# Last down-projection steps by columns, shorter norm sums, down loads in order of use, and the first head's q and k staged earlier

## The chip, the cores and the metric

The kernel runs on one core of one Trainium2 chip. The core has TensorE (matmuls and transposes, called PE in the profile), VectorE (DVE), ScalarE (ACT), GpSimd (POOL) and SyncE (SP, which here only issues DMAs). SBUF is the working memory, PSUM holds the results of matmuls. The metric is device time in microseconds of one execution, and lower is better; several runs are given by their median.

## The reference, cut to what matters

A trunk of two layers over 1024 rows of width 1024, in float32. Layer 0 mixes rows by a gated block, layer 1 by attention of 16 heads; each then has a gated ConvFFN with its own norm before it, and a final norm ends the trunk.

```python
def rmsnorm(x, g):
    return x * lax.rsqrt(jnp.mean(x * x, axis=-1, keepdims=True) + EPS) * g

def conv_ffn(h, w_in, conv_w, conv_b, w_down):          # D_FF = 2816
    a = causal_conv3(h @ w_in, conv_w) + conv_b
    up, gate = jnp.split(a, 2, axis=-1)
    return (jax.nn.silu(gate) * up) @ w_down

h = x
h = h + gmlp_mixer(rmsnorm(h, a_norm_g), ...)            # mixer A
h = h + conv_ffn(rmsnorm(h, f_norm_g[0]), ...)
k, v = jnp.split(rmsnorm(h, kv_norm_g) @ w_kv, 2, -1)
h = h + chunk_attention(rmsnorm(h, b_norm_g), k, v, w_q, rel_bias, w_o)
h = h + conv_ffn(rmsnorm(h, f_norm_g[1]), ...)
return rmsnorm(h, final_norm_g)
```

## The kernel before

**Layout and precision.** The residual `h` lies transposed in SBUF: eight tiles of 128 features by 1024 rows, handled as two halves of 512 rows, t = 0 and t = 1. A float32 operand is split into a rounded high part (`whi`, `yh`: a copy on ScalarE, L137) and the rest (`wlo`, `yl`: a subtraction, L138, mostly on VectorE), and a product takes three matmuls: high by high, low by high, high by low.

**Order of the work.** TensorE's instructions run in the order of the program text. Of the other engines and of SyncE's queue the program's scheduler sets the order when the kernel is built, except in blocks marked `manual_schedule`. Work that must not hold TensorE up is put off: `put_off(us, fn)` runs `fn` when a clock that counts the matmuls issued so far (`tick`: columns/2400 us + 0.0025) has passed that many us. `tc.issue_after(ins)` puts the block's instructions behind `ins` on that engine.

**Norms.** For each half, `square_sum` squares every new tile of `h` on ScalarE (L217, L220) and adds the squares into two tiles `acc[0]` and `acc[1]`, odd tiles on VectorE and even ones on GpSimd. `rstd_rows` adds the two on VectorE (L226), and 0.9 us of the clock later TensorE sums over the features with four small products (L231, eight matmul instructions, `pm`). The mean (L197), the power -1/2 on GpSimd (L198), a diagonal tile (L204) and a product with ones (`bc`, L207) follow, then the scaled tiles `y` (L243) and their splits.

**Down projection.** `down` multiplies by one level of a seven-product block scheme: seven products p in the order 1, 6, 2, 7, 5, 4, 3, each with 11 steps q, 77 steps in all. A step is twelve matmuls of 512 columns: four output blocks m ("columns" here), each three matmuls, into four PSUM banks. Two steps' operands come with one pair of loads on SyncE (L799 for the weights' part `d`, L800 for the activations' part `g`) into eight buffers; the splits are made some three steps ahead, and the pair `whi`, `wlo` has four buffers. For the first 24 steps ScalarE, VectorE and SyncE keep the text's order; after that the scheduler's. When p = 4 ends, half t = 0 of `h` is complete and `after(0, ...)` starts its norm during p = 3; when p = 3 ends, half t = 1 is. In layer 0 that is the norm for attention, in layer 1 the final norm.

**The first head.** After layer 0's `down`, TensorE makes the first pair of heads' q, k, v of t = 0, then v, q, k of t = 1. Then `first` splits them (L960 to L967), and `stage(0)` copies them by six DMAs (L999) into the operand tiles QE, QS, KM, KS. The pass for the row maxima (`Max`, L1021 to L1032) reads them first.

**The end.** In the final norm `rows` transposes blocks of `h` back (`back`, L1283), scales and stores (`store`, L1288). For t = 1, `gain` makes transposed blocks times the gain beforehand, and `last` scales and stores them.

Of the kernel before, what the change touches and what calls it, by code (L numbers as in the profile page):

```python
# [46 lines left out]
def trunk(ctx: ExitStack, tc: tile.TileContext, x, a_win, a_wv, a_wst, a_bs, a_wout, w_kv, w_q, w_o,  # L47
# [174 lines left out]

    def rstd_rows(acc, pool, then, n=4):

        cs = slice(0, n * P)
# [40 lines left out]
    def norm(h, acc, t, gain, ys):  # L266
# [8 lines left out]
        put_off(4.2 if t else 3.2, lambda: rstd_rows(acc, npl, lambda r: put_off(2.9 if t else 6.0, lambda: scale(r))))  # L275
# [18 lines left out]
    def norm_first(h, acc, gain, X):  # L294
# [11 lines left out]
        put_off(3.2, lambda: rstd_rows(acc, npl, lambda r: put_off(6.0, lambda: scale(r))))  # L306

    def norm_second(h, acc, gain, X):
# [40 lines left out]
        put_off(4.6, lambda: rstd_rows(acc, npl, lambda r: put_off(3.6, lambda: scale(r))))  # L349
# [38 lines left out]
    with tc.tile_pool(name="a1", bufs=1, reuse_waits="tile") as a1, \  # L388
# [152 lines left out]
        def out_a(t, gs, room=None):  # L541
            hs = halves[t]
            acc = new_acc(npl)
# [238 lines left out]
    def down(l, gs, ds, hold, after):  # L782

        wd = f_wdown[l].rearrange("(q e p) c -> p q e c", e=2, p=P)
        with tc.tile_pool(name=f"dx{l}", bufs=4, reuse_waits="tile") as dx, \
# [4 lines left out]
            ready, raw, sets = [], {}, [0]  # L790

            def load(p, q):
# [6 lines left out]
                nc.sync.dma_start(d[:, :n, :], src[p] if p in src else ds[LEFT[p]][:, q:q + n, :])  # L799
                nc.sync.dma_start(g[:, :n, :], gs[RIGHT[p]][:, q:q + n, :])  # L800
# [13 lines left out]
            s1, acc = [None] * 4, [None, None]  # L814
            bank = {b: [psum[n][i][:, hs] for hs in halves for n in ("up", "gate")] for i, b in enumerate("ab")}
            for n, (p, q) in enumerate(steps):
# [8 lines left out]
                (wh, wl), (xh, xl) = ready[n]  # L825
                ready[n] = True
                b = "a" if p in (1, 2, 5, 3) else "b"
                first, last = q == 0 and p in (1, 6, 5, 4), q == NP - 1
# [5 lines left out]
                if not last:  # L834
                    continue
# [59 lines left out]
    for what in "qkv":  # L895
        proj(ps2[what, 0], w2[what], ys[0])
# [515 lines left out]
```

## Time and profile before

| what | value |
|---|---|
| median of 3 runs | 2236.21 us (2229.96 to 2240.26) |
| the profiled execution: its own time | 2239.42 us |
| its span in the trace | 2237.2 us |
| mean granted clock of TensorE | 0.988 |
| busy in the span: PE, DVE, ACT, POOL | 2162.8, 1583.7, 1081.2, 728.2 us |

A profile is of one execution: the span goes from its first instruction to its last, and the time of the execution is 2.2 us longer. The rows of the trace count us from the start of the span. The stages lie as follows: mixer A to about 300 us, layer 0's ConvFFN to 736, its `down` to 960, first q, k, v to 1005, attention to 1500, its output product to 1560, layer 1's ConvFFN to 1994, its `down` to 2219, then the end.

### The profile page before, as it was taken

Reading aid. Unit: us, or ns where it says so; the run is one execution under the profiler, and the core shown is the slowest. Engines: PE = TensorE matmul, PEld = TensorE weight load, DVE = VectorE, ACT = ScalarE, POOL = GpSimd, SP = SyncE. Lnnn points to the kernel's source line nnn. Section 1 sums busy time; section 2 is a strip of 40 time slices with the busy share of each in tenths; the row PEclk is TensorE's granted clock in tenths of the full one; section 3 lists DMA queues with packets and bytes.
Section 4 is the critical chain, followed back from the end, with each engine's and each line's share of the span. In section 5 each row is a group of like instructions: output and inputs, shape, how many; then the busy total and the mean of one; then the engine's idle time right before and its main releaser. Section 6 shows DMA issues by size and latency. Waiting matters only on the chain.

```text
span 2237.2 us, 28258 instructions
## 1 busy us (share of the span) xinstructions
PE 2162.8 (97%) x9880; PEld 1785.8 (80%) x9880; DVE 1583.7 (71%) x2406; ACT 1081.2 (48%) x1909; POOL 728.2 (33%) x487
## 2 busy tenths in 40 slices
PE   8999999999999999998999999999999999999997
PEld 7888887888888887777888888787778888888876
DVE  4763869888888665654767776664988888885555
ACT  6544445454454543444555555552544444455432
POOL 0311316424234112153444444352543333240111
PEclk9999999999999999999999999999999999999998
DMA  5242224444445865335444444653244444477652
GB/s 203 85 141 76 90 99 146 168 144 164 143 170 186 316 234 189 122 116 125 109 113 115 113 123 123 179 170 152 85 160 168 148 162 162 156 255 278 211 174 80
DMA packets 151054, 344.04 MB, mean 154 GB/s; under 512 B 31744, under 2 KB 32128, under 8 KB 150912
## 3 DMA queue, kind: packets, MB, share of 16 engines
q1 hardware_dynamic: 148176, 337.31, 46.4%
q10 hardware_dynamic: 2736, 4.93, 0.6%
q8 instruction: 77, 1.26, 0.2%
q14 instruction: 65, 0.53, 0.1%
HBM read 225.20 MB, written 87.56 MB: 140 GB/s over the span
## 4 chain that ended last, share of the span: by engine, by line
PE 48%; DVE 20%; issue 18%; DMA 8%; POOL 3%; ACT 3%; SPq 0%; DVEq 0%; ACTq 0%; POOLq 0%
DVE wlo L138 6%; PE vps L468 4%; DMA raw<-in_f_win 3%; PE up L357 3%; PE up L359 3%; PE up L362 3%; DVE a L707 3%; PE qkv L186 3%; PE qkv L182 2%; PE qkv L179 2%; PE gate L357 2%; PE gate L359 2%; DVE S L372 2%; PE gate L362 2%; PE up L832 2%
## 5 line engine op out<-in xcount | busy, mean ns | idle before, releaser
L138 DVE TENSOR_TENSOR wlo<-raw,whi 128x512 fp32r<-128x512 f32 x425 | 370.0, 888 | 181.4 <-ACT whi L137 181.1
L137 ACT CAST whi<-raw 128x512 fp32r<-128x512 f32 x429 | 262.7, 626 | 231.4 <-PE gate L832 110.3
L357 PE MATMUL up<-yh,whi 128*128 128x512 f32 x688 | 269.9, 392 | 6.8 <-ACT gate L760 6.6
L359 PE MATMUL up<-yh,wlo 128*128 128x512 f32 x688 | 268.0, 390 | 0.0
L1081 POOL TENSOR_TENSOR pl<-p,ph 128x640 fp32r<-128x640 f32 (+4 forms) x128 | 163.8, 1283 | 203.6 <-ACT ph L1080 109.9
L721 POOL TENSOR_TENSOR h<-a 128x512 f32<-128x512 f32 x44 | 80.1, 1820 | 368.2 <-DVE a L713 368.2
L357 PE MATMUL gate<-th,whi 128*128 128x512 f32 x496 | 193.4, 390 | 5.0 <-DVE gate L774 3.1
L359 PE MATMUL gate<-th,wlo 128*128 128x512 f32 x496 | 193.0, 389 | 0.0
L138 DVE TENSOR_TENSOR yl<-raw,yh 128x512 fp32r<-128x512 f32 x180 | 126.1, 734 | 94.1 <-ACT yh L137 93.9
L362 PE MATMUL up<-yl,whi 128*128 128x512 f32 x688 | 184.5, 389 | 0.5 <-POOL yl L138 0.5
L137 ACT CAST yh<-raw 128x512 fp32r<-128x512 f32 x184 | 105.8, 617 | 117.9 <-DMA raw<-gT 95.2
L357 PEld LDWEIGHTS up<-yh,whi 128*128 128x128 f32 x688 | 129.1, 188 | 40.9 <-ACT gate L760 14.3
L362 PEld LDWEIGHTS up<-yl,whi 128*128 128x128 f32 x688 | 129.1, 188 | 28.3 <-POOL yl L138 1.3
L359 PEld LDWEIGHTS up<-yh,wlo 128*128 128x128 f32 x688 | 129.2, 188 | 26.3
L182 PE MATMUL qkv<-yh,wlo 128*128 128x512 f32 x336 | 134.8, 401 | 0.0
L179 PE MATMUL qkv<-yh,whi 128*128 128x512 f32 x336 | 133.0, 396 | 0.0
L362 PE MATMUL gate<-tl,whi 128*128 128x512 f32 x496 | 132.6, 389 | 0.0
L137 ACT CAST whi<-S 128x512 fp32r<-128x512 f32 x160 | 99.0, 620 | 63.3 <-PE up L362 58.1
L832 PE MATMUL up<-yh,wlo 128*128 128x512 f32 x308 | 122.0, 396 | 6.7 <-DVE wlo L138 6.6
L832 PE MATMUL up<-yh,whi 128*128 128x512 f32 x308 | 121.6, 395 | 1.8 <-ACT whi L137 1.8
L138 DVE TENSOR_TENSOR wlo<-S,whi 128x512 fp32r<-128x512 f32 x160 | 121.3, 759 | 0.0
L832 PE MATMUL up<-yl,whi 128*128 128x512 f32 x308 | 121.2, 394 | 0.0
(253 smaller groups left out, 5330.6 us busy)
## 6 DMA issues: line engine op xcount, KB each, us to landing
raw<-in_f_win SPq DMA_DIRECT2D x88, 512.0 KB, 3.6
gT<-h SPq DMA_DIRECT2D x88, 256.0 KB, 2.7
h<-in_f_wdown SPq DMA_DIRECT2D x44, 512.0 KB, 4.5
dS<-h SPq DMA_DIRECT2D x88, 256.0 KB, 2.1
raw<-dS SPq DMA_DIRECT2D x40, 512.0 KB, 3.5
raw<-gT SPq DMA_DIRECT2D x40, 512.0 KB, 5.2
gB<-a SPq DMA_DIRECT2D x66, 256.0 KB, 2.1
raw<-in_f_wdown SPq DMA_DIRECT2D x30, 512.0 KB, 5.4
```

Source lines behind the costliest of these rows:

```text
L137: S.copy(hi, src)
L138: return eng.tensor_tensor(lo, src, f32(hi), op=ALU.subtract)
L179: nc.tensor.matmul(ps, wh[:, k, :], xs[k][0], start=k == 0, stop=False)
L182: nc.tensor.matmul(ps, wl[:, k, :], xs[k][0], start=False, stop=False)
L186: nc.tensor.matmul(ps, wh[:, k, :], xs[k][1], start=False, stop=k == last)
L357: nc.tensor.matmul(ps, wh[:, k, :], xs[k][0], start=first and k == 0, stop=False, skip_group_check=True)
L359: nc.tensor.matmul(ps, wl[:, k, :], xs[k][0], start=False, stop=False, skip_group_check=True)
L362: nc.tensor.matmul(ps, wh[:, k, :], xs[k][1], start=False, stop=k == 3, skip_group_check=True)
L468: nc.tensor.matmul(ps, a, b, start=k == i == 0, stop=k == KD - 1 and i == 2)
L721: G.tensor_tensor(B[n], x, B.get(y) if isinstance(y, str) else y, op=ALU.subtract)
L832: nc.tensor.matmul(ps, w[:, ms], x, start=first and i == 0, stop=last and i == 2, skip_group_check=True)
L1081: marks[2] = G.tensor_tensor(pl[:, :n], pf[:, :n], f32(ph[:, :n]), op=ALU.subtract)
```

## The change

Five edits. (1) `square_sum` leaves only tile 2's addition on GpSimd, merges the two sums when tile 6 is in, and adds tile 7 to the merged sum; `rstd_rows` has no addition and no delay of its own, and the times of its callers are new. (2) In layer 1 the last four steps of p = 3 are done column by column, twelve matmuls to a column, and each column's result is added to `h` and squared right behind it (`whole`). (3) Each pair of down loads is put behind the pair before it in SyncE's queue. (4) The first head's operand tiles are opened before its q, k, v; half t = 0 of q and k is split and staged ahead of the products of t = 1, half t = 1 right behind them, and KM goes first. (5) In the end, the four `gain` blocks of t = 1 are made during p = 3, `last` scales them on ScalarE and stores them from ScalarE's queue, and the other four go through `rows` on VectorE and SyncE's queue.

`operand`, `stage` and `constant_rows` are moved out of the attention block with little change; lines that only move are cut.

```diff
@@ -207,31 +207,28 @@
-    def new_acc(pool, bufs=2):
-        return [pool.tile([P, H], F32, tag="acc", name="acc", bufs=bufs) for _ in range(2)]
+    accs = [2]
 
     def square_sum(acc, h, m, pool):
 
-        a = acc[m % 2][:, 0:h.shape[1]]
         if m < 2:
-            S.activation(a, h, AF.Square)
-        else:
-            sq = pool.tile([P, H], F32, tag="f", name="sq")[:, 0:h.shape[1]]
-            S.activation(sq, h, AF.Square)
-            (V if m % 2 else G).tensor_tensor(a, a, sq, op=ALU.add)
-
-    def rstd_rows(acc, pool, then, n=4):
-        behind["sum"] = V.tensor_tensor(acc[0][:, cs], acc[0][:, cs], acc[1][:, cs], op=ALU.add)
-
-        def rows():
-            pt = psS("pm")
-            for i in range(n):
-                nc.tensor.matmul(pt[:, i:i + 1], acc[0][:, i * P:(i + 1) * P], ones[:, 0:1], start=True, stop=True)
-                tick(0)
-            then(rstd_of(pt[:, :n], n, pool))
-        put_off(0.9, rows)
+            acc.append(pool.tile([P, H], F32, tag="acc", name="acc", bufs=accs[0]))
+            S.activation(acc[m], h, AF.Square)
+            return
+        sq = pool.tile([P, H], F32, tag="f", name="sq")
+        S.activation(sq, h, AF.Square)
+        a = acc[0 if m == KD - 1 else m % 2]
+        (G if m == 2 else V).tensor_tensor(a, a, sq, op=ALU.add)
+        if m == KD - 2:
+            V.tensor_tensor(a, a, acc[1], op=ALU.add)
+
+    def rstd_rows(acc, pool, then):
+
+        pt = psS("pm")
+        for i in range(4):
+            nc.tensor.matmul(pt[:, i:i + 1], acc[0][:, i * P:(i + 1) * P], ones[:, 0:1], start=True, stop=True)
+            tick(0)
+        then(rstd_of(pt[:, :4], 4, pool))
...
-        put_off(4.2 if t else 3.2, lambda: rstd_rows(acc, npl, lambda r: put_off(2.9 if t else 6.0, lambda: scale(r))))
+        put_off(8.5 if t else 6.0, lambda: rstd_rows(acc, npl, lambda r: put_off(2.9 if t else 6.0, lambda: scale(r))))
...
-        put_off(3.2, lambda: rstd_rows(acc, npl, lambda r: put_off(6.0, lambda: scale(r))))
+        put_off(4.0, lambda: rstd_rows(acc, npl, lambda r: put_off(6.0, lambda: scale(r))))
...
-        put_off(4.6, lambda: rstd_rows(acc, npl, lambda r: put_off(3.6, lambda: scale(r))))
+        put_off(3.6, lambda: rstd_rows(acc, npl, lambda r: put_off(3.2, lambda: scale(r))))
...
+            end = 4 if l else 1
...
-                nc.sync.dma_start(d[:, :n, :], src[p] if p in src else ds[LEFT[p]][:, q:q + n, :])
-                nc.sync.dma_start(g[:, :n, :], gs[RIGHT[p]][:, q:q + n, :])
+                with tc.issue_after(behind["down"].ins) if sets[0] > 1 else ExitStack():
+                    nc.sync.dma_start(d[:, :n, :], src[p] if p in src else ds[LEFT[p]][:, q:q + n, :])
+                    behind["down"] = nc.sync.dma_start(g[:, :n, :], gs[RIGHT[p]][:, q:q + n, :])
...
+            s1, acc = [None] * 4, [[], []]
+
+            def whole(p, m, ps):
...
+                V.tensor_tensor(x, ps, x, op=ALU.add)
+                square_sum(acc[t], x, k, npl)
...
+                if n > len(steps) - end:
+                    continue
+                todo = range(n, n + end if n == len(steps) - end else n + 1)
                 for m in range(4):
                     ps, ms = bank[b][m], slice(m * P, (m + 1) * P)
-                    for i, (w, x) in enumerate(((wh, xh), (wl, xh), (wh, xl))):
-                        nc.tensor.matmul(ps, w[:, ms], x, start=first and i == 0, stop=last and i == 2, skip_group_check=True)
-                        tick()
-                if not last:
+                    for k in todo:
+                        q = steps[k][1]
+                        (wh, wl), (xh, xl) = ready[k]
+                        for i, (w, x) in enumerate(((wh, xh), (wl, xh), (wh, xl))):
+                            nc.tensor.matmul(ps, w[:, ms], x, start=q == i == 0 and p in (1, 6, 5, 4),
+                                             stop=q == NP - 1 and i == 2, skip_group_check=True)
+                            tick()
+                    if q == NP - 1 and len(todo) > 1:
+                        whole(p, m, ps)
+                for k in todo:
...
+                if len(todo) == 1:
+                    for m in range(4):
+                        whole(p, m, bank[b][m])
...
+    bt_ctx, b0_ctx = ExitStack(), ExitStack()
+    bt = bt_ctx.enter_context(tc.tile_pool(name="bt", bufs=2, reuse_waits="tile"))
+    b0 = b0_ctx.enter_context(tc.tile_pool(name="b0", bufs=1, reuse_waits="tile"))
+
+    QE, QS, KM, KS = ([b0.tile([P, T], F32R, name=f"{n}0")] for n in ("qe", "qs", "km", "ks"))
+
+    def constant_rows(c, places):
+        oth = rows[c][1]
+        for tl, off in ((QE[c], P), (KM[c], P + T)):
+            for hs in halves:
+                e = places()
+                nc.sync.dma_start(e[oth], consts[oth, off + hs.start:off + hs.stop])
+                S.copy(tl[oth, hs], e[oth])
...
+        if what == "q":
+            S.mul(hi[:, hs], ps, 0.125)
+            V.scalar_tensor_tensor(lo[:, hs], ps, 0.125, f32(hi[:, hs]), op0=ALU.mult, op1=ALU.subtract)
+        elif what == "k":
+            S.copy(hi[:, hs], ps)
+            V.tensor_tensor(lo[:, hs], ps, f32(hi[:, hs]), op=ALU.subtract)
...
+    def stage(hd, cs=slice(0, T)):
+
+        p, c = divmod(hd, 2)
+        own, oth = rows[c]
+        q, k = parts[p, "q"], parts[p, "k"]
+        if cs.start == 0:
+            G.memset(f32(QE[c][own.stop % P:own.stop % P + 1, :]), 0.0)
+        for dst, src in ((KM[c][own], k[0]), (QE[c][own], q[0]), (QS[c][own], q[0]), (QS[c][oth], q[1]),
+                         (KS[c][own], k[1]), (KS[c][oth], k[0])):
+            nc.sync.dma_start(f32(dst[:, cs]), f32(src[own, cs]))
+
+    def first(what, t):
+
+        for _ in operand(0, what, None, t):
+            pass
...
-    w2 = {"q": weights(0, "q"), "k": weights(0, "k"),
-          "v": weights(0, "v", wv_ctx.enter_context(tc.tile_pool(name="wv", bufs=1, reuse_waits="tile")))}
+    wv = wv_ctx.enter_context(tc.tile_pool(name="wv", bufs=1, reuse_waits="tile"))
+    w2 = {what: weights(0, what, wv if what == "v" else None) for what in "qkv"}
     for what in "qkv":
         proj(ps2[what, 0], w2[what], ys[0])
+    constant_rows(0, lambda: wv.tile([P, H], F32, tag="e", name="e", bufs=4))
+    first("q", 0)
+    first("k", 0)
+    stage(0, halves[0])
     proj(psv[:, H:T], w2["v"], ys[1])
     for what in "qk":
         ps2[what, 1] = psS("qk")
         proj(ps2[what, 1], w2[what], ys[1])
+        first(what, 1)
+    stage(0, halves[1])
...
+        constant_rows(1, lambda: b2.tile([P, H], F32, tag="o", name="e"))
...
-        def first(what, t):
-            for _ in operand(0, what, w2[what], t):
-                pass
-        for what, t in (("q", 0), ("k", 0), ("q", 1), ("k", 1), ("v", 0), ("v", 1)):
-            first(what, t)
-        stage(0)
+        for t in range(2):
+            first("v", t)
...
-    def store(n, i, j, o):
-        nc.sync.dma_start(out[n * H + i * P:n * H + (i + 1) * P, halves[j]], o)
+    def store(n, i, j, o, queue=nc.sync):
...
-        gained = {}
-
-        def gain(i, j):
-            ps = back(1, i, j)
-            gained[i, j] = new_o()
-            V.tensor_tensor(gained[i, j], ps, fg[j], op=ALU.mult)
+        def gain(i):
+
+            ps = back(1, i, 1)
+            gained.append(new_o())
+            V.tensor_tensor(gained[i], ps, fg[1], op=ALU.mult)
 
         def last(r):
             for i in range(4):
-                for j in (1, 0):
-                    if (i, j) not in gained:
-                        gain(i, j)
-                    o = gained[i, j]
-                    if j:
-                        V.tensor_scalar(o, o, r[:, i:i + 1], None, op0=ALU.mult)
-                    else:
-                        S.mul(o, o, r[:, i:i + 1])
-                    store(1, i, j, o)
+                S.mul(gained[i], gained[i], r[:, i:i + 1])
+                store(1, i, 1, gained[i], nc.scalar)
+                rows(r, i, 0)
         if n:
-            put_off(0.5, lambda: [gain(i, 1) for i in range(4)])
             put_off(1.6, lambda: rstd_rows(acc, npl, last))
         else:
-            put_off(3.2, lambda: rstd_rows(acc, npl, lambda r: [
+            put_off(6.0, lambda: rstd_rows(acc, npl, lambda r: [
                 put_off(2.9 + 0.6 * i, lambda i=i: rows(r, i // 2, i % 2)) for i in range(8)]))
+            for i in range(4):
+                put_off(16.0 + 0.8 * i, lambda i=i: gain(i))
```

## Rows read from the trace of the kernel before

**Rows 1.** Waits of TensorE, 800 to 1030 us: engine, line, releaser: total us, times, longest.
```profile
PE mx L1021 <- DMA km<-thi: 6.5, 1, 6.5
PE pm L231 <- DVE acc L226: 5.7, 2, 3.5
PE up L832 <- DVE wlo L138: 3.6, 6, 1.8
PE up L832 <- ACT whi L137: 0.9, 1, 0.9
```
**Rows 2.** The same view, 1690 us to the end.
```profile
PE pm L231 <- DVE acc L226: 7.2, 2, 4.8
PE up L832 <- DVE wlo L138: 3.0, 5, 1.5
```
**Rows 3.** The same view, whole span.
```profile
PE gate L357 <- DVE gate L774: 3.1, 2, 1.6
```
**Rows 4.** Busy time by stretch: us, each engine (x instructions), granted clock, DMA share, GB/s.
```profile
750.00:800.00 50.00, 50.00 (x222) 41.40 (x222) 26.13 (x40) 23.58 (x42) 5.19 (x5) 1.00 0.83 304
898.00:905.00 7.00, 5.16 (x16) 3.79 (x15) 4.82 (x8) 3.22 (x6) 1.27 (x1) 0.76 0.94 330
928.00:936.00 8.00, 5.81 (x23) 4.44 (x22) 4.15 (x6) 0.70 (x2) 1.87 (x2) 0.79 0.17 51
957.00:968.00 11.00, 9.42 (x34) 6.99 (x33) 6.89 (x8) 4.75 (x8) 7.80 (x4) 0.84 0.61 203
968.00:981.00 13.00, 9.48 (x31) 7.17 (x30) 7.01 (x7) 0.68 (x2) 8.66 (x5) 0.74 0.43 140
1009.00:1021.00 12.00, 5.50 (x18) 4.28 (x17) 1.45 (x8) 0.60 (x1) 1.90 (x1) 0.72 1.02 232
2184.00:2192.00 8.00, 5.60 (x22) 4.39 (x21) 4.09 (x6) 0.88 (x2) 1.80 (x2) 0.79 0.11 33
2229.00:2237.00 8.00, 1.99 (x10) 1.59 (x8) 3.54 (x8) 2.67 (x4) 0.00 (x0) 0.50 0.69 262
```
**Rows 5.** Timeline, SyncE's queue and ScalarE, 860 to 880 us: start, us, instruction [idle before].
```profile
862.35 2.19 SPq L799 DMA_DIRECT2D raw<-in_f_wdown  x2
865.86 6.23 SPq L800 DMA_DIRECT2D raw<-gT  x2
875.48 2.18 ACT L137 CAST yh<-raw 128x512 fp32r<-128x512 f32 x4 [9.44 <-DMA raw<-gT]
```
**Rows 6.** Timeline of VectorE and GpSimd, 2179 to 2189 us.
```profile
2183.56 2.57 DVE L221 TENSOR_TENSOR acc<-acc,sq 128x512 f32<-128x512 f32 x2
2186.65 0.69 DVE L226 TENSOR_TENSOR acc<-acc 128x512 f32<-128x512 f32 x1
2181.79 2.99 POOL L221 TENSOR_TENSOR acc<-acc,sq 128x512 f32<-128x512 f32 x2 [23.80 <-ACT sq L220]
```
**Rows 7.** Timeline of VectorE, TensorE and SyncE's queue, 2216 us to the end.
```profile
2218.50 1.29 DVE L850 TENSOR_TENSOR h<-up,h 128x512 f32<-128x512 f32 x2 [8.85 <-PE up L832]
2220.90 2.48 DVE L1309 TENSOR_TENSOR o<-fin,fg 128x512 f32<-128x512 f32 x4
2224.87 0.69 DVE L226 TENSOR_TENSOR acc<-acc 128x512 f32<-128x512 f32 x1
2225.71 1.77 PE L231 MATMUL pm<-ones,acc 128*128 128x1 f32 x8 [4.81 <-DVE acc L226]
2229.59 4.47 SPq L1288 DMA_DIRECT2D out<-o  x8
```
**Rows 8.** Timeline of VectorE, 968 to 992 us; SyncE's queue at 1009; ScalarE at 2208.
```profile
981.17 1.88 DVE L243 TENSOR_TENSOR y<-h,bc 128x512 f32<-128x512 f32 x3 [3.17 <-PE bc L207]
989.92 0.69 DVE L138 TENSOR_TENSOR yl<-y,yh 128x512 fp32r<-128x512 f32 x1 [0.69 <-ACT yh L137]
...
1009.54 1.04 SPq L999 DMA_DIRECT2D km<-thi  x1
...
2208.30 0.62 ACT L137 CAST whi<-raw 128x512 fp32r<-128x512 f32 x1 [2.10 <-PE gate L832]
```

More of the change, by code (lines that the diff above doesn't have):

```diff
@@ L812, in make @@
                 ready.append((w, x))
-            s1, acc = [None] * 4, [None, None]
+            s1, acc = [None] * 4, [[], []]
+            def whole(p, m, ps):
+                (h11, h12), (h21, h22) = ([h[i][:, hs] for hs in halves] for i in (m, m + 4))
+                if p == 1:
+                    s1[m] = du.tile([P, H], F32, tag="s1", name="s1", bufs=4)
+                    S.copy(s1[m], ps)
+                    return
+                if p in (6, 7):
+                    u = du.tile([P, H], F32, tag="u", name="u")
+                    V.tensor_tensor(u, ps, s1[m], op=ALU.add)
+                    for x in ((h12,) if p == 6 else (h21, h22)):
+                        G.tensor_tensor(x, x, u, op=ALU.add)
+                    return
+                x, t, k = {2: (h11, 0, m), 5: (h22, 1, m), 4: (h21, 0, m + 4), 3: (h12, 1, m + 4)}[p]
+                V.tensor_tensor(x, ps, x, op=ALU.add)
+                square_sum(acc[t], x, k, npl)
+            accs[0] = 4
             bank = {b: [psum[n][i][:, hs] for hs in halves for n in ("up", "gate")] for i, b in enumerate("ab")}
@@ L885, in trunk @@
     osave = dp.tile([2, KD, P, T], F32, name="osave")
+    rows = [(slice(0, 64), slice(64, P)), (slice(64, P), slice(0, 64))]
     def weights(p, what, pool=None):
@@ new lines, in trunk, with operand @@
+    parts = {}
+    def operand(p, what, w, t):
+        hs = halves[t]
+        if t == 0:
+            if what == "v":
+                parts[p, what] = [b1.tile([P, NB, 64], F32R, tag=f"v{n}", name=f"v{n}") for n in ("hi", "lo")]
+            else:
+                parts[p, what] = [bt.tile([P, T], F32R, tag=f"t{n}", name=f"t{n}") for n in ("hi", "lo")]
+        hi, lo = parts[p, what]
+        if p == 0:
+            ps = ps2[what, t]
+        else:
+            ps = psP("qkv")
+            yield from products(ps, w, ys[t], range(KD), LAST)
+        if what == "q":
[4 more added lines that the diff above has]
+            V.tensor_tensor(lo[:, hs], ps, f32(hi[:, hs]), op=ALU.subtract)
+        else:
+            vT = b2.tile([P, H], F32, tag="vT", name="vT")
+            S.copy(vT, ps)
+            put_off(1.2, lambda: transpose_v(vT, t, hi, lo))
@@ L910, in trunk @@
     os_ = [[None] * KD, [None] * KD]
-    rows = [(slice(0, 64), slice(64, P)), (slice(64, P), slice(0, 64))]
     def psO(name):
@@ L989, in transpose_v @@
                 V.tensor_tensor(vl, src, f32(vh), op=ALU.subtract)
-        def stage(hd):
-            p, c = divmod(hd, 2)
-            own, oth = rows[c]
-            q, k = parts[p, "q"], parts[p, "k"]
-            G.memset(f32(QE[c][own.stop % P:own.stop % P + 1, :]), 0.0)
-            for dst, src in ((QE[c][own], q[0]), (KM[c][own], k[0]), (QS[c][own], q[0]), (QS[c][oth], q[1]),
-                             (KS[c][own], k[1]), (KS[c][oth], k[0])):
-                nc.sync.dma_start(f32(dst), f32(src[own]))
         def stage_v(p):
@@ L1285, in back @@
         return ps
-    def store(n, i, j, o):
-        nc.sync.dma_start(out[n * H + i * P:n * H + (i + 1) * P, halves[j]], o)
+    def store(n, i, j, o, queue=nc.sync):
+        queue.dma_start(out[n * H + i * P:n * H + (i + 1) * P, halves[j]], o)
     def new_o():
         return yp.tile([P, H], F32, tag="yh", name="o")
+    gained = []
     def final(n, acc):
```

66 lines of the change are left out of this document (9 added, 57 removed).

## The prediction

> **What bounds the kernel now.** TensorE is busy 2162.8 of 2237.2 us, so 74 us are idle, and only what takes idle time away, or the slow matmuls behind it, can help. I read the granted clock first (0.988), then TensorE's waits, then the busy time by stretch around each wait, then the timelines of the engine that each wait names. Three kinds of wait lie where the change works: the products `pm` wait for the sums of squares, the matmuls of `down` wait for split weights, and the first head's row maxima wait 6.5 us for one copy of k [rows 1, 2]. The reader is to see that the waits are late hand-overs, one after the other, and not a lack of throughput: in the first part of `down` TensorE does 222 matmuls in 50 us without a gap [rows 4], so the pace is 0.225 us.
>
> A wait costs more than its idle time. In the stretches with the longer waits the granted clock averages 0.72 to 0.84 instead of 1.00 [rows 4], a mean over the levels 2.4 and 1.2 GHz, and matmuls at the lower one take twice as long. So I price each wait by its stretch: length minus starts times the pace, where a `pm` product counts 0.11 us (eight take 1.77 us in the end, where the clock stands at 0.50 [rows 4, 7]) and a `bc` product 0.45, my estimate, as two ordinary ones.
>
> - a, `pm` in layer 0's p = 3: 8 us, 15 matmuls and 8 `pm`: 8 - 3.4 - 0.9 = 3.7 lost.
> - b, the same in layer 1: 14 and 8: 8 - 3.2 - 0.9 = 3.9.
> - c, `pm` of t = 1 behind layer 0's `down`: 21, 8 and 2 `bc`: 13 - 4.7 - 0.9 - 0.9 = 6.5.
> - d, the first q weights: 11 - 34 x 0.225 = 3.3.
> - e, the row maxima: 12 - 18 x 0.225 = 7.9 [all rows 4].
>
> **Sums (edit 1).** VectorE's last group gets five additions where it had three (tiles 4 and 6 come from GpSimd; the merge moves ahead of tile 7). At 0.6 us a place that is 1.2 us more. Against this, VectorE's two additions took 2.57 us while GpSimd's two ran for 2.99 beside them [rows 6]; two clean ones in a row take 1.29 [rows 7], so 1.3 us come back when GpSimd's go. By the count alone the sum is ready 1.2 us later, with that excess gone about as early as now.
>
> The Trainium skill, SBUF — State Buffer, Who interferes with whom, says that a VectorE instruction with two SBUF inputs and a GpSimd instruction that reads SBUF exclude each other. By that rule the excess goes whole and the total below would be about 0.6 higher; by the bare count it would be 2.4 lower. The trace agrees with the rule in the 2.57 against 1.29.
>
> The products themselves move on the clock from 3.2 + 0.9 to 6.0, some 2.0 us of matmuls. The idle times are 5.7 - 3.5 = 2.2 for a and 7.2 - 4.8 = 2.4 for b [rows 1, 2], so 0.2 and 0.4 us stay idle, with the sums as early as now: a and b give 3.5 each. Should the sums come 1.2 us later, about half of each price stays, so each lies between 1.5 and its whole price.
>
> For c the products move from 5.1 to 8.5, 3.6 us against an idle 3.5 [rows 1]: the 6.5 go. But `bc` now comes 53 matmuls into the 72 of t = 0, and 19 matmuls, 4.3 us, lie between it and the product that reads the new tiles. Making the eight tiles took from 981.17 to 990.61 [rows 8]; the last one's high part, some 8.8 us behind `bc`, is wanted after 14 more matmuls, at 7.5. That puts back 1.3 us: c gives 5.2, between 3 (the tiles another 2 us later, since the first head's splits are now on the same engines) and 6.5.
>
> d keeps its chain: a buffer freed by the last split of `down`, the load, the gain, the split. All that moves earlier with TensorE. If it did not, the wait would grow by what a gives. I take 0, with -3 to +3. For the other norms, `norm_second` starts 2.3 us of the clock earlier, and VectorE is then behind in the ConvFFN, where TensorE waits 3.1 us for it [rows 3]; half of it, 1.5, with 0 to 3.1 (term j).
>
> **Loads in order (edit 3).** ScalarE sits 9.44 us idle before four casts for one `gT` load: its queue was filled with two weight loads at 862.35, and the second `gT` came 6 us behind the first [rows 5]. The weight casts queued behind these casts then are late, and TensorE waits. Where the order of use holds by hand, in the first 24 steps, there is no wait: 222 matmuls in 50 us at a DMA share of 0.83 [rows 4]. In layer 0 the waits are 3.6 + 0.9; the longest, 1.8, lies in a stretch that loses 7 - 16 x 0.225 = 3.4, so 6.1 in all (f) [rows 1, 4]; in layer 1 they are 3.0 (g) [rows 2]. Some of them stand beside GpSimd's long additions at the ends of p = 7 and p = 5, which stay; I take two thirds: 4.0 and 2.0, with 0 and all as the bounds.
>
> **The first head (edit 4).** The copy of k was issued at 1009.54 [rows 8] and ended the wait about 7 us later. The maxima begin on half t = 0, whose copies now go out some 20 us ahead. Block 4 is the first to want t = 1, 3.4 us behind block 0; k's last product ends near 1005, so a copy issued at 1006 lands about 1013, just ahead of that. If the queue holds it to 1009.54 again, 3.1 us of wait and a slow stretch come back. e lies between 3.4 and 7.9; I take 6.4, as VectorE's work on eight blocks is what is late next. The four casts and four subtractions for q and k were there before, and so were the constant rows; they only come earlier, under 24 matmuls each (5.4 us) of products.
>
> **The end (edits 2 and 5).** From the first addition at 2218.50 to `pm` at 2225.71 pass 7.2 us: four additions to `h`, four `gain` multiplications of 2.48, squares, and the sums [rows 7]. By columns one addition, one square and one sum stay behind the last matmul: about 0.7 + 0.6 + 0.7, 0.3 for handing over, and 0.5 because the first addition had not waited for the last bank, 2.8 in all: 4.4 saved. `pm` may keep the full clock, 0.9; I count 0.6. Eight stores of 256 KB are 2.1 MB, at 262 GB/s [rows 4] 8 us, which is all the time from the first issue at 2229.59 [rows 7] to the end at 2237.2: so the end follows the first store, and h is 5.0, between 4 and 6.5 (if the issuing, 4.47 us on one queue [rows 7], were what counts).
>
> The Trainium skill, DMA: Bandwidth & Descriptors, Issuing engines are not separate DMA queues, says that issuing from a second engine saves issue time only, because all run on the same 16 DMA engines. By it the 6.5 isn't reached. No row of before has two queues at once in the end.
>
> The sixteen transposes of `gain` were hidden under that wait; in p = 3 they cost TensorE 16 x 0.11 = 1.8 (term i). The column order needs step 76's weights nine matmuls, 2.0 us, behind step 72, whose buffer they take: a cast of 0.62 [rows 8] and a subtraction of 0.69 [rows 6] make 1.3. It is hidden with 0.7 to spare; without the cover it costs 1 us.
>
> **Sum.** 3.5 + 3.5 + 5.2 + 0 + 6.4 + 4.0 + 2.0 + 5.0 - 1.8 + 1.5 = 29.3 us off 2239.42, the profiled execution, gives 2210.1. The median of the runs is 3.2 below that execution, so I predict 2207. All upper bounds together give 3.7 + 3.9 + 6.5 + 3 + 7.9 + 6.1 + 3.0 + 6.5 - 1.8 + 3.1 = 42, all lower ones 1.5 + 1.5 + 3 - 3 + 3.4 + 0 + 0 + 4 - 1.8 + 0 = 9.
>
> **Rivals.**
> 1. The next thing is late. The loads' order frees nothing (f and g 0), the new tiles and the second half of k come late (c 3, e 3.4), d grows by 3: 3.5 + 3.5 + 3 - 3 + 3.4 + 5.0 - 1.8 + 1.5 = 15, 2221. For it: VectorE is busy 7 of 13 us in c's stretch and the copies' queue was full. Against it: the pauses are of several causes, which need not all move.
> 2. Slower: strict order blocks SyncE's queue. A weight load waits for a buffer that TensorE's pace frees, the `g` load behind it waits too, and every pair comes late. With 27 pairs behind step 24 in each `down` a wait of 1 us a pair is 54 us: with f and g 0, 2236 - 23 + 54 = 2267. It turns the sign from 23 / 54 = 0.43 us a pair. For it: the 9.44 us [rows 5] show how far one late load reaches. Against it: the first 24 steps run so without a gap [rows 4].
> 3. The loads were not the cause, the rest holds: f and g 0, 2213, inside the range.
>
> **How the numbers follow.** Forecast and rival 3 together 0.65 (its own range 2196 to 2215), rival 1 0.22, rival 2 0.07, no change that shows 0.06. The range is 2195 to 2226: from the upper bounds to rival 1 with its spread. A measurement of this kernel tells about 0.5%, 11 us, from no change: faster 0.84 (a few cases of rival 1 fall short), same 0.10, slower 0.06.
>
> **What would show it.** Right: no wait of `pm` over 1 us, none of `mx` for `km` over 3, weight waits in `down` below 3 us in all, `pm` in the end some 2.5 us behind the last matmul. Wrong: loads further apart with TensorE waiting at every second step; waits of `v` for `yh`, or of the maxima's transposed row for VectorE, of several us; or a longer attention stage, which the change does not touch but whose order the scheduler makes anew, and which this sum leaves as it is.

## The result

The changed kernel takes 2215.36 us (median of 5 runs, 2211.32 to 2221.08) against 2236.21 (5 runs, 2229.96 to 2240.26): a ratio of 0.9912 with a 95% interval of 0.9888 to 0.9935, some 20 us. The forecast was 2207. The profiled execution took 2217.12 us; its span is 2215.3, the granted clock 0.993, TensorE is busy 2152.2 us.

**The profile after.** First the waits of TensorE over the whole span (engine, line, releaser: us in total, times, longest), to be held against [rows 1 to 3].

```profile
PE up L853 <- DVE wlo L138: 10.1, 6, 2.7
...
PE gate L354 <- ACT h L695: 5.5, 4, 2.1
...
PE pm L229 <- DVE acc L221: 4.6, 3, 2.3
...
PE qk L179 <- ACT whi L137: 2.3, 1, 2.3
...
PE mx L1054 <- DMA km<-thi: 1.5, 1, 1.5
PE v L179 <- ACT yh L137: 1.5, 3, 0.6
...
PE qk L182 <- DVE wlo L138: 1.3, 1, 1.3
```

The first head's wait for `km`, 6.5 us before, is gone: the 1.5 us above stand at 1400 us, in a later head. The waits of `pm` are down from 12.9 to 4.6 us. But `up` waits 10.1 us for `wlo`, more than the 6.6 before [rows 1, 2], and the tiles of t = 1 are late three times (`v` for `yh`). The end, on VectorE, TensorE and the two queues that store (start, us, instruction, idle before it):

```profile
2201.73 0.68 DVE L829 TENSOR_TENSOR h<-gate,h 128x512 f32<-128x512 f32 x1
2203.17 0.69 DVE L221 TENSOR_TENSOR acc<-acc,sq 128x512 f32<-128x512 f32 x1 [0.76 <-ACT sq L219]
...
2204.01 1.02 PE L229 MATMUL pm<-ones,acc 128*128 128x1 f32 x8 [2.32 <-DVE acc L221]
...
2207.19 3.02 SPq L1317 DMA_DIRECT2D out<-o  x4
...
2208.39 1.78 ACTq L1317 DMA_DIRECT2D out<-o  x2
```

One addition and one sum stand behind the last matmul, and `pm` waits 2.32 us where it waited 4.81 [rows 7]. From `pm` to the end pass 11.3 us (2204.01 to 2215.3), before 11.5.

Where the time went, stage by stage. The bounds are the starts of the first or last matmul of a kind; the last column is the prediction's sum for the stage.

| stage | before | after | difference | predicted |
|---|---|---|---|---|
| ConvFFN, layer 0 | 435.5 | 433.3 | -2.3 | j, 1.5 for both |
| `down`, layer 0 | 223.4 | 224.4 | **+1.0** | **-7.5 (a, f)** |
| from there to the last q, k, v product | 45.2 | 43.5 | -1.7 | -5.2 (c, d) |
| to the first product of the maxima | 12.1 | 5.4 | -6.7 | -6.4 (e) |
| to the first transposed row `mr` | 10.0 | 7.6 | -2.4 | with e |
| attention behind it, to its last `st` | 453.0 | 451.5 | -1.5 | 0 |
| to the ConvFFN of layer 1 | 78.5 | 78.8 | +0.3 | 0 |
| ConvFFN, layer 1 | 436.3 | 435.2 | -1.1 | j |
| `down`, layer 1 | 224.2 | 221.7 | -2.5 | -3.7 (b, g, i) |
| the end | 18.5 | 14.0 | -4.5 | -5.0 (h) |

With 0.7 us ahead of the first stage this makes 21.9, the difference of the spans. A stage is known to some 3 us, and more where the scheduler's order decides, for it makes that order anew in each kernel: in the ten kernels below with the same text there, layer 0's ConvFFN takes 432.7 to 436.2 us. The 8.5 us missing in layer 0's `down` stand out, and the experiments begin there. The stages of a run are those of one execution, which can lie some us off the run's median (most of all in e2, e5, e9 and e10, where it is said).

### The profile page after: what moved, and what is told of

It is laid out like the page before. It is cut to its first block, busy times and chain, and to the rows that moved or that the text cites. A ratio compares the mean times of both kernels' runs of the same rounds, so it can differ in the third digit from the quotient of the medians.

```text
span 2215.3 us, 28221 instructions
## 1 busy us (share of the span) xinstructions
PE 2152.2 (97%) x9880; PEld 1781.0 (80%) x9880; DVE 1584.9 (72%) x2418; ACT 1083.0 (49%) x1909; POOL 686.0 (31%) x471
## 4 chain that ended last, share of the span: by engine, by line
PE 48%; DVE 20%; issue 13%; DMA 11%; ACT 4%; POOL 2%; SPq 1%; POOLq 0%; DVEq 0%; ACTq 0%
DVE wlo L138 6%; DMA raw<-gT 5%; PE vps L465 4%; PE up L354 4%; PE up L356 4%; PE up L359 4%; PE gate L354 3%; PE gate L356 3%; PE gate L359 3%; DMA raw<-in_f_win 3%; DVE yl L138 2%; PE qkv L186 2%; PE qkv L182 2%; PE qkv L179 2%; DVE a L704 2%
## 5 line engine op out<-in xcount | busy, mean ns | idle before, releaser
L718 POOL TENSOR_TENSOR h<-a 128x512 f32<-128x512 f32 x44 | 75.4, 1714 | 367.5 <-DVE a L710 350.3
L853 PE MATMUL up<-yh,wlo 128*128 128x512 f32 x308 | 122.1, 396 | 10.1 <-DVE wlo L138 10.1
L369 POOL TENSOR_TENSOR h<-h 128x512 f32<-128x512 f32 x44 | 80.5, 1844 | 140.9 <-DMA h<-in_f_wdown 116.4
```

Source lines behind the costliest of these rows:

```text
L369: eng.tensor_tensor(A[n], a, b, op=op)
L718: G.tensor_tensor(B[n], x, B.get(y) if isinstance(y, str) else y, op=ALU.subtract)
L853: nc.tensor.matmul(ps, w[:, ms], x, start=q == i == 0 and p in (1, 6, 5, 4), stop=q == NP - 1 and i == 2, skip_group_check=True)
```

## The experiments

Each ratio is to the kernel before, run beside it; the changed kernel's is 0.9912. An interval is about 0.002 wide to either side, 4 us, so a stage's length and the ratio are read together.

**e1: the changed kernel without the fixed order of loads.**

```diff
-                with tc.issue_after(behind["down"].ins) if sets[0] > 1 else ExitStack():
```

> The changed kernel without the fixed order of down's loads; all else as changed. In the changed kernel's profile down takes 224.4 us in layer 0 and 221.7 in layer 1, against 223.4 and 224.2 before. Theory A (the order decides nothing; the late weight splits come from the queues of ScalarE and VectorE and from the few buffers): 224 and 222 within 1, the whole at 2215 within 4. Theory B (the order itself costs and took back what the earlier products gave): layer 0's down 219 to 221, the whole near 2210. Theory C (the prediction's: the order gains 4.0 and 2.0, something else lost them): 228 and 224, the whole near 2221.

Ratio 0.9866 (0.9848 to 0.9884), 2209.2 us. `down` takes 217.0 and 221.0 us. That is theory B: the order cost 7.4 us in layer 0; the 0.7 in layer 1 is within what a stage is known to. Behind layer 0's `down` the products of q, k and v take 40.5 us instead of 43.5, and layer 0's ConvFFN is 2.9 longer, so the 8.5 us between the two spans are not `down` alone. TensorE's waits for splits from 730 to 1010 us, in the changed kernel and in e1:

```profile
PE up L853 <- DVE wlo L138: 7.2, 4, 2.7
...
PE up L853 <- ACT whi L137: 0.9, 1, 0.9
```
```profile
PE up L852 <- DVE wlo L138: 2.5, 3, 1.4
...
PE up L852 <- ACT whi L137: 1.0, 1, 1.0
```

**e2: the kernel before with the order alone.** The same line, put in.

> The kernel before with the fixed order of down's loads alone. Theory A: down takes 223.4 and 224.2 us within 1, as before, and the ratio to before is 1.000 within 0.002. Theory B: layer 0's down 226 to 228, the ratio 1.001 to 1.003. Theory C: 219 and 222, the whole 6 us shorter, ratio 0.997.

Ratio 1.0011 (0.9999 to 1.0023); `down` takes 227.2 and 226.0 us, 3.8 and 1.7 longer. The ratio excludes C (0.997): the order alone gains nothing. It doesn't tell B from A (1.000). The stages speak for B, but weakly: the profiled execution is the longest of the twelve, 6 us above their median, and its ConvFFN of layer 0, which the edit doesn't touch, is some 3 us longer too.

**Where the order costs.** Counted by steps, the changed kernel loses 1.9 of the 7.4 us against e1 up to the end of p = 7 (a first wait of 1.3 us stands at 843), 2.4 in the eight steps behind it, nothing in the next six, and 3.1 from there to the end, where `up` waits 2.7 us at 902 and `pm` 1.6 in p = 3. The stretch behind the end of p = 7 has the most waits in a short time, 862 to 872 us (busy time of TensorE, its weight loads, VectorE, ScalarE, GpSimd, then clock and DMA), in the changed kernel and in e1:

```profile
862.00:872.00 10.00, 5.90 (x22) 4.23 (x21) 9.97 (x11) 3.21 (x6) 8.60 (x6) 0.92 0.25 92
```
```profile
862.00:872.00 10.00, 9.35 (x40) 7.10 (x39) 8.17 (x10) 2.33 (x5) 8.89 (x6) 1.00 0.48 157
```

22 matmuls against 40: 18 x 0.225 = 4.0 us, with VectorE busier and GpSimd about as busy. (It is more than the 2.4 because e1 has a wait of 1.6 us for the next splits at 878, which the changed kernel has not.) The queues of the changed kernel at this place (SyncE, ScalarE, VectorE, GpSimd):

```profile
856.57 0.32 SPq L798 DMA_DIRECT2D raw<-dS  x1
857.17 0.32 SPq L799 DMA_DIRECT2D raw<-gT  x1
857.54 0.42 SPq L798 DMA_DIRECT2D raw<-in_f_wdown  x1
858.01 0.47 SPq L799 DMA_DIRECT2D raw<-gT  x1
868.63 0.38 SPq L798 DMA_DIRECT2D raw<-in_f_wdown  x1
871.99 0.32 SPq L799 DMA_DIRECT2D raw<-gT  x1
...
864.45 1.14 ACT L137 CAST yh<-raw 128x512 fp32r<-128x512 f32 x2 [1.94 <-DMA raw<-gT]
...
863.83 1.37 DVE L138 TENSOR_TENSOR wlo<-raw,whi 128x512 fp32r<-128x512 f32 x1
865.13 3.48 DVE L138 TENSOR_TENSOR yl<-raw,yh 128x512 fp32r<-128x512 f32 x2
868.53 0.68 DVE L824 TENSOR_TENSOR u<-up,s 128x512 f32<-128x512 f32 x1
869.13 1.15 DVE L138 TENSOR_TENSOR wlo<-raw,whi 128x512 fp32r<-128x512 f32 x1
...
863.40 12.65 POOL L826 TENSOR_TENSOR h<-h,u 128x512 f32<-128x512 f32 x8 [32.10 <-DVE u L824]
```

And e1, the same queues:

```profile
854.56 0.32 SPq L798 DMA_DIRECT2D raw<-gT  x1
855.76 0.32 SPq L797 DMA_DIRECT2D raw<-dS  x1
856.97 0.32 SPq L798 DMA_DIRECT2D raw<-gT  x1
...
860.48 1.66 ACT L137 CAST yh<-raw 128x512 fp32r<-128x512 f32 x3 [4.15 <-DMA raw<-gT]
...
861.13 1.29 DVE L138 TENSOR_TENSOR yl<-raw,yh 128x512 fp32r<-128x512 f32 x2 [3.59 <-ACT yh L137]
...
862.94 0.68 DVE L138 TENSOR_TENSOR yl<-raw,yh 128x512 fp32r<-128x512 f32 x1
...
864.14 2.87 DVE L138 TENSOR_TENSOR wlo<-raw,whi 128x512 fp32r<-128x512 f32 x2
```

With the order, the loads of two sets go out in one burst and the second `gT` leaves at 858.01; without it at 856.97, although e1's `down` began 3.2 us later. It is also under way longer: the casts that wait for it begin 6.4 us after its issue in the changed kernel, 3.5 in e1. So in the changed kernel ScalarE casts the second set's two `yh` at 864.45, VectorE's two `yl` come at 865.13, beside GpSimd's additions, where one takes 1.74 us, and the second `wlo`, for which TensorE waits, comes at 869.13 behind them. In e1 three `yl` are through by 863.6, just as GpSimd begins (863.11), at 0.6 to 0.7 us each, and two `wlo` follow in a row.

The Trainium skill, SBUF — State Buffer, Who interferes with whom, says that VectorE contends with GpSimd's reads when both its inputs come from SBUF, and not, outside its two-port modes, with one input from there. The trace agrees: beside the same additions a `u` sum (868.53), which reads one bank of PSUM, stays at 0.68 us, the splits go from 0.69 to 1.74.

**e8: the order kept, g ahead of d.**

```diff
-                    nc.sync.dma_start(d[:, :n, :], src[p] if p in src else ds[LEFT[p]][:, q:q + n, :])
-                    behind["down"] = nc.sync.dma_start(g[:, :n, :], gs[RIGHT[p]][:, q:q + n, :])
+                    nc.sync.dma_start(g[:, :n, :], gs[RIGHT[p]][:, q:q + n, :])
+                    behind["down"] = nc.sync.dma_start(d[:, :n, :], src[p] if p in src else ds[LEFT[p]][:, q:q + n, :])
```

> The changed kernel with the fixed order of down's loads kept, but g issued ahead of d in each set. Theory B1 (the order costs because g's load stands behind d's, and d's buffer comes free later, with the low part of the weights, than g's): with g ahead, layer 0's down comes down from 224.4 us to 217 to 220, the whole to 2209 to 2212. Theory B2 (any fixed order costs, since a set of loads must wait for the whole set before it): down stays at 222 to 225, the whole at 2215 within 4.

Ratio 0.9862 (0.9846 to 0.9877), 2208.4 us; `down` takes 216.1 and 220.5. So B1's numbers hold: it is not that any order costs. How `d` holds `g` up is less plain. The waits of SyncE's queue, 850 to 872 us, first in the changed kernel, where L798 is the load of `d` and L799 that of `g`:

```profile
SPq L798 <- DMA raw<-gT: 12.3, 2, 6.3
SPq L798 <- DVE yl L138: 6.1, 2, 4.2
SPq L799 <- DVE wlo L138: 3.2, 2, 3.0
```

and in e8, where L798 is the load of `g` and L799 that of `d`:

```profile
SPq L798 <- DMA raw<-gT: 9.9, 2, 5.2
SPq L798 <- DVE yl L138: 5.5, 2, 3.5
SPq L799 <- DVE yl L138: 3.9, 1, 3.9
SPq L799 <- DMA raw<-gT: 3.3, 1, 3.3
SPq L799 <- DVE wlo L138: 0.2, 1, 0.2
```

The longest waits of both queues are for an earlier `gT` to land. Of the waits for a buffer, those with `d` ahead end with `yl` for `d` and with `wlo` for `g`, so B1's wording had the buffers the wrong way round: `d` takes the one that comes free first, and `g`, which the casts want first, stands behind it, up to 3.0 us. In e8 `g` waits for `yl`, and it is `d` that stands behind. But those 3.0 us lie at 869 to 872 us, too late to cause the waits of TensorE at 865 and 870; the `g` load issued at 857.17 waited only 0.3 for its buffer. The trace points to a second way in which `d` delays `g`: the transfer itself. Over the `g` loads behind step 24 of layer 0 the time from issue to landing averages 5.1 to 5.6 us in the kernels that fix the order with `d` ahead (the changed one, e2 to e5, e7), 4.7 to 4.8 in those without an order (the one before, e1, e9), and 4.4 to 4.5 with `g` ahead (e8, e10). No run parts the place in the queue from the transfer. e1, left to the scheduler, issues a `gT` first too, at 854.56.

**e5: without GpSimd's additions to `h`.** The last two lines of the branch for p = 6 and 7 go.

> The changed kernel, fixed order and all, but GpSimd's additions to h at the ends of p = 6 and 7 are left out (the output is not the reference's). Theory G (the late loads hurt because the splits then fall into GpSimd's additions, where VectorE's take 1.8 us instead of 0.7): the waits of up for wlo at the end of p = 7, 4.1 us in the changed kernel, are below 1 us, layer 0's down is 219 to 221 and layer 1's 219 to 221. Theory H (the loads are late by themselves): the waits stay above 3 us, layer 0's down is 223 to 225.

2209.9 us (0.9873, 0.9855 to 0.9891); `down` takes 220.3 and 220.1 us, in a profiled execution that is 5.5 us above the median. The wait behind the end of p = 7, 4.1 us in the changed kernel, is down to 0.5 (first line, 850 to 875 us), but behind the end of p = 5 it is longer than the 2.7 of the changed kernel (second line, 875 to 905):

```profile
PE up L851 <- DVE wlo L138: 0.5, 1, 0.5
...
PE up L851 <- DVE wlo L138: 3.8, 3, 3.4
```

So G holds at one place and H at the other: GpSimd adds nothing to `h` at the end of p = 5, and late loads are enough there. The edit also takes away VectorE's own waits for GpSimd, which must have read `u` before VectorE writes it again (1.8 us at 869 us in e1), so it doesn't test the contention alone.

**e9: no order, the twelve additions on VectorE.**

```diff
-                        G.tensor_tensor(x, x, u, op=ALU.add)
+                        V.tensor_tensor(x, x, u, op=ALU.add)
```

> The changed kernel without the fixed order, and with the twelve additions to h at the ends of p = 6 and 7 on VectorE instead of GpSimd. Theory G: without GpSimd beside them VectorE's splits keep 0.7 us; twelve additions of 0.6 us are 7.2 us more on VectorE, which is idle for 4 us and more between sets; layer 0's down, 217.0 us in the run without the order, becomes 215 to 216.5, the whole 2206 within 4. Rival (VectorE's queue is the bound at the end of p = 7; eight additions of 0.6 us put the splits behind them off by 4.8 us): a wait of up for wlo of 3 us or more at that place, down 219 to 222, the whole 2213.

Ratio 0.9868 (0.9851 to 0.9884): as e1. `down` takes 215.4 and 218.6, and TensorE does 46 matmuls from 862 to 872 us, but the median doesn't tell it from e1; the profiled execution, with a span of 2201.1 us, is the shortest of its five runs (2202.9 to 2212.4). With the loads in time, the contention is worth little.

**e3: the first head placed late.** The early calls of `first` and `stage` go, the old ones behind the last product come back.

> The changed kernel with the first head's q and k made, split and copied where they were before, behind the last product; all else as changed. Theory (the early copies take the waits out of the first row maxima, worth 9 us between the start of down's successor and the first row): the first row maximum comes 7 us later than in the changed kernel, the attention's first stage again has a wait of mx for km of 5 to 7 us, the whole is 2222 to 2225. Rival (the wait is only moved, and the attention catches up behind it): the first maximum is 7 us later, but the last stage of the attention less than 3, the whole is 2217.

Ratio 0.9943 (0.9926 to 0.9960), 7 us above the changed kernel's. From the last matmul of layer 0's `down` to the first maximum 55.0 us pass instead of 48.9, to the first `mr` 65.0 instead of 56.5, and the attention's last `st`, counted from the same matmul, is 8.2 later: the delay isn't caught up, the rival falls. The wait is back:

```profile
PE mx L1049 <- DMA km<-thi: 5.9, 1, 5.9
```

**e4: the sums' products at the old times.**

```diff
-        put_off(8.5 if t else 6.0, lambda: rstd_rows(acc, npl, lambda r: put_off(2.9 if t else 6.0, lambda: scale(r))))
+        put_off(5.1 if t else 4.1, lambda: rstd_rows(acc, npl, lambda r: put_off(2.9 if t else 6.0, lambda: scale(r))))
...
-        put_off(3.6, lambda: rstd_rows(acc, npl, lambda r: put_off(3.2, lambda: scale(r))))
+        put_off(5.5, lambda: rstd_rows(acc, npl, lambda r: put_off(3.6, lambda: scale(r))))
...
```

> The changed kernel with the four waiting times ahead of the sums' products as they were before (4.1, 5.1, 5.5 and 4.1 us of the clock in all); the shortened sums, the order of loads, the head and the end as changed. Theory D (each wait has its own price): the waits of pm come back, layer 0's down gets 3 to 4 us longer (228), layer 1's 3 to 4 (225), the products behind layer 0's down 3 to 5, ConvFFN 2 to 3; the whole 2228. Theory E (in layer 0's down another thing is late right behind, so that its wait of pm costs nothing): down 224 and 225, the products 3 to 5 longer, the whole 2224. Theory F (the shortened sums did the work and not the times): no wait of pm above 1 us, the whole 2216.

Ratio 0.9946 (0.9929 to 0.9963), 7 to 8 us above. No theory holds throughout. Layer 1's `down` is 5.7 us longer (D), but so it is by 4.8 in e3, which has the new times, so that says little. Layer 0's is 222.8: `pm` waits 2.7 us in p = 3 and nothing is lost against the changed kernel, as E has it; but its waits for splits are 4.5 us where the changed kernel has 8.1, so what the 2.7 cost isn't shown. And behind layer 0's `down` the stage is 44.2 us against 43.5, where D and E had 3 to 5 more:

```profile
PE qk L179 <- ACT whi L137: 2.8, 1, 2.8
PE pm L229 <- DVE acc L221: 1.3, 1, 1.3
PE qk L182 <- DVE wlo L138: 1.0, 1, 1.0
```

At the old times `pm` waits 1.3 us here, not 3.5 [rows 1]. Its sum isn't earlier (`pm` starts 14.1 us behind the end of `down`, before 13.4): the first q weights are later, 3.8 us in all instead of 1.4 + 0.2 before, and that wait covers the sum.

**e7: the end by steps.** `end = 1` in both layers.

> The changed kernel with the last four steps of layer 1's down in the order of steps and not of columns; the products with gain stay early, the sums shortened, the stores on two queues. Theory I (the order by columns carries the end): from the last matmul of down to the sums' products the wait is 4 us or more instead of 2.3, and from there to the end as before; the stage from down's last stretch to the end is 2 to 3 us longer. Rival (the early products with gain carry it, the columns nothing): the wait stays at 2.3 to 3 us, the end within 0.7 us of the changed kernel's.

Ratio 0.9919 (0.9905 to 0.9934). The stage from the last matmul of `down` to the end is 18.0 us instead of 14.0. Theory I, and a little more: the wait is 3.0 us longer, and the slower products behind it (1.84 us, in the changed kernel 1.02) and what follows give the last 1. The whole doesn't show it: the ratio is the changed kernel's within its interval, since other stages came out shorter.

```profile
2206.47 1.84 PE L229 MATMUL pm<-ones,acc 128*128 128x1 f32 x8 [5.31 <-DVE acc L221]
```

**e10: g first, the additions on VectorE, t = 1's products at 6.6 instead of 8.5.**

> The changed kernel with g ahead of d in the fixed order, the twelve additions to h on VectorE, and the products for the sums of t = 1 at 6.6 us of the clock instead of 8.5. If the three add up: layer 0's down 214 to 215 (its waits of up for wlo, 2.6 us with g ahead, are gone), layer 1's down 218 to 220 against 221.7, the products behind layer 0's down 1 to 1.5 shorter because the tiles of t = 1 are no longer late (1.98 us lost at three places), the whole 2204 within 4. Rival (VectorE carries 7 us more in each down and is the next thing late; the products of t = 1 wait for the sum): a wait of up for wlo or of pm for acc of 2 us or more, the whole 2209 or above.

Ratio 0.9849 (0.9833 to 0.9866), 2201.3 us, `down` 215.6 and 215.8, and between the first and the last q product 39.0 us instead of e8's 41.6. The sum holds by the median, not stage by stage: layer 1's `down` was expected at 218 to 220. A wait of 1.6 us for `wlo` is left at 866 us. Its profiled execution is again the shortest (span 2193.9), and its attention stage, which the edits don't touch, is 4.5 us shorter than e8's.

**e11: g first, and the written order kept for 52 steps.**

```diff
-                if n == 24:
+                if n == 52:
                     entry.close()
```

> The changed kernel with g ahead of d, and with the written order on ScalarE, VectorE and SyncE kept for 52 of down's 77 steps instead of 24. If the scheduler's order of the splits is what makes them late behind step 24: no wait of up for wlo or whi above 0.5 us up to step 52, which takes in the ends of p = 6, 2 and 7, layer 0's down 213 to 215, the whole 2205. Rival (the additions at the ends of the groups, written behind the splits' loads, stand in line ahead of splits that are wanted sooner, and the copies that wait for a load hold all behind them): waits of 3 us or more at the ends of p = 2 and 7, layer 0's down 220 or more, the whole 2213 or above.

Ratio 0.9843 (0.9825 to 0.9860), 2199.5 us; `down` takes 212.4 and 216.9. The largest wait in either, but for the last sum, is 0.4 us; from 850 to 905 us, where the changed kernel waits 6.8, this is all, and below it what e8 has there:

```profile
PE up L853 <- DVE yl L138: 0.5, 2, 0.3
```
```profile
PE up L853 <- DVE wlo L138: 2.6, 2, 1.8
```

The rival falls, though `u` does stand in line for GpSimd. By the ratio alone e11 isn't told from e8; by the waits it is.

**e12 and e14: the same with t = 1's products at 6.6, and with the written order to the end.** e14 leaves out the two lines that close it.

> The run with g ahead of d and the written order kept for 52 steps, and the products for the sums of t = 1 at 6.6 us of the clock instead of 8.5. If the late tiles of t = 1 (0.36 + 0.81 + 0.81 us lost at three places of that run) follow the products' time: one place of them is left, the stage from the first q product to the last 1 us shorter, 38.7 us instead of 39.8, the whole 2198 to 2200. Rival (the sum of t = 1 isn't ready at 6.6, and the products wait for it): a wait of pm for acc of 1 us or more in this stage, which stays at 39.8 or gets longer.

> As the run beside it, with the written order kept to the end of down (all 77 steps). If the written order is as good behind step 52 as ahead of it: nothing late in down but the last sum, the whole within 3 us of the run beside it. Rival (at the ends of p = 4 and 3 the squares and the first norm's work, written where the clock puts them, hold up splits): waits of up for whi or wlo, or of pm, of 2 us or more behind p = 5, the whole 4 us or more above the run beside it.

e12: ratio 0.9831 (0.9805 to 0.9856), 2196.8 us, the fastest here; the first q product to the last takes 38.6 us, one late tile is left. That it beats e11 the median doesn't show. e14: 0.9891 (0.9865 to 0.9917), its rival: `pm` waits 2.0 us in each p = 3, `bc` 0.9, and three waits for operands of 1.3, 0.4 and 1.8 us stand in the last steps of layer 0; `down` is 221.7 and 222.5 us.

VectorE in e12 at the place looked at above (p = 7 ends at 854.7 us in both kernels), and the same ten microseconds:

```profile
857.58 0.69 DVE L824 TENSOR_TENSOR u<-up,s 128x512 f32<-128x512 f32 x1 [1.97 <-POOL h L826]
860.10 0.69 DVE L824 TENSOR_TENSOR u<-gate,s 128x512 f32<-128x512 f32 x1 [1.82 <-POOL h L826]
860.70 1.16 DVE L138 TENSOR_TENSOR wlo<-raw,whi 128x512 fp32r<-128x512 f32 x1
861.79 1.78 DVE L138 TENSOR_TENSOR yl<-raw,yh 128x512 fp32r<-128x512 f32 x1
863.49 1.78 DVE L138 TENSOR_TENSOR wlo<-raw,whi 128x512 fp32r<-128x512 f32 x1
```
```profile
862.00:872.00 10.00, 9.42 (x41) 7.15 (x40) 9.79 (x11) 3.43 (x6) 4.42 (x3) 1.00 0.53 167
```

The contention is all there, 1.78 us for a split. But each step's `wlo` comes ahead of its `yl`, and no later step's splits stand before it; TensorE does 41 matmuls.

## Why the prediction was right or wrong

The sign and the range were right, and the whole is 8 us short of the forecast. The time lies near rival 3's 2213, and that is chance: f was not 0 but a loss, and others made up for part of it (the first head gave 2.7 us more than its term, the attention and the ConvFFNs some 3 more than theirs, which is within what such stages vary by). Two of the prediction's own signs failed: the waits for splits in `down` are 11.0 us where it asked for less than 3, and `pm` in layer 0 waits 1.6 where it asked for 1 at most. Term by term:

**f and g, the loads in order (4.0 and 2.0): wrong, and the step that failed.** The prediction said that "where the order of use holds by hand, in the first 24 steps, there is no wait", and took from it that order on SyncE's queue removes the waits. But in those steps ScalarE and VectorE follow the written order too. e11 shows what that counts for, beside e8, which differs in that alone: kept on all three, the waits for splits in layer 0 fall from 2.6 to 0.5 us. Kept on SyncE alone with `d` ahead, as here, they grew from 4.5 to 8.1. The prediction also put GpSimd's long additions at the ends of p = 7 and p = 5; the program has them at the ends of p = 6 and p = 7, and the wait behind p = 5 stays without them (e5). Layer 0's `down` takes 222.3 to 227.2 us in the five kernels of this kind that do all the work (the changed one, e2, e3, e4, e7), and 215.4 to 217.0 in the changed kernel without an order or with `g` ahead (e1, e8 to e10); layer 1's 221.7 to 227.3 and 215.8 to 221.0. The bounds "0 and all" left a loss out. It was in rival 2, whose mechanism, the `g` load held up behind `d`, came true in part and at a quarter of its price: 7.4 us over 27 pairs is 0.27 us a pair, and TensorE waits for splits at four places in layer 0, not at every pair. Rival 3 stopped at nothing gained.

**a and b, `pm` in p = 3 (3.5 each): right in kind, covered in layer 0.** Without the order layer 0's `down` is 6.4 us shorter than before (e1). That holds a and, besides, a wait of `up` at the end of p = 5 that fell from 1.84 to 1.38 us; before, the clock stood at 0.76 around it [rows 4], in e1 at 1.00 (895 to 902 us). In the changed kernel `pm` still waits 1.6 us in layer 0 and 0.7 in layer 1. In layer 1 b, g and i together gave 2.5 in the changed kernel and 3.3 without the order (e1); with e3 and e4 as far apart from it as they are, they can't be told one from the other.

**c and d (5.2 and 0): mis-sized, 1.7 together.** The wait of `pm` went, as predicted, and the tiles of t = 1 came late, as predicted (0.36 + 0.81 + 0.81 us lost against the 1.3 put back). What was missed is d: the first q weights are 3.6 us late where they were 1.6, inside d's range but not the 0 of the sum. With 8.5 as the time the rest was given away: at 6.6, e12 has one late tile left and is 1.2 us shorter in this stage than e11.

**e (6.4): right, a little small.** 6.7 us to the first maximum and 2.4 more to the first `mr`, 9.1; e3 puts 8.5 of it back. Nothing else was late in its place: from 945 to 1032 us TensorE has no wait of the maxima left.

**h (5.0): right.** 4.5, of which e7 puts 4.0 on the columns. That two queues for the stores gave anything isn't shown. The Trainium skill, DMA: Bandwidth & Descriptors, Issuing engines are not separate DMA queues, has only issue time to be saved that way; the trace agrees: SyncE issues four stores in 3.0 us where it issued eight in 4.47 [rows 7], and from `pm` to the end pass 11.3 us instead of 11.5, and 12.3 in e7, which has the two queues as well and slower `pm` products.

**j (1.5): not told.** Before, the ConvFFNs take 435.5 and 436.3 us; with the new time for the norm they take 432.7 to 436.2 and 433.3 to 436.1 in eleven profiles. The wait of `gate` for VectorE [rows 3] went, but those for ScalarE's `h`, 1.9 us in all before (0.9 the longest), are now 5.5 (2.1), so the term's wait was in part moved and not removed.

**Open.** By which of the two ways `d` ahead delays `g`, its buffer or its transfer, isn't parted. Whether the written order with `d` ahead would also be free of waits wasn't tried, nor `down` with more than two `u` buffers. Why the first q weights come later in most of these kernels isn't settled: in e1 and e12 TensorE waits only for their low part (1.9 and 1.3 us), in the changed kernel, e8 and e9, with the order and without, for both.

## What to carry to other kernels

An order fixed on one queue isn't the order by hand that worked elsewhere: look which engines were held in the stretch that served as evidence. Here holding the queue alone cost 7.4 us with one load ahead and nothing with the other, and holding all three engines was best. Where two loads share one queue and its buffers, issue first what the next engine reads first: the second waits in line, and lands later. Of a wait taken away, ask what stands directly behind it: in layer 0 the 3.5 us of `pm` came out only once the splits were in time.

## What the runs showed of the hardware

A split of 512 columns on VectorE takes 0.69 us alone and 1.74 to 1.78 beside GpSimd's additions, while a sum with one operand in PSUM stays at 0.68 in the same microseconds. And the length of a wait alone doesn't tell what becomes of the clock: around a wait of 1.38 us it stayed at 1.00 over seven us (e1, 895 to 902), around one of 1.84 us at the same place before it averaged 0.76 [rows 4], and around one of 2.69 us there in the changed kernel it stayed at 1.00 again (900 to 915).
